# The gated unit of the S5 branch: from the end of the projection stage into the recurrence's stage, in halves of the tokens

## The chip, the cores and the metric

The kernel runs on one core of a Trainium2 chip, in fp32. The metric is the device time of one execution in microseconds; smaller is better. The core's engines are PE (matrix products), DVE (element-wise work and scans), ACT (functions and copies), POOL (element-wise work) and SP (issues most DMAs). Each engine runs its instructions strictly in order. DMAs are issued from SP's queue, and some from those of ACT and POOL.

## The reference

One layer of 1024 tokens and 2048 features. After an adaptive layer norm, a product with `w_in` makes the inputs of three branches: an S5 state space branch (512 features), a pooling branch (512) and an RWKV7 recurrence (1024, two directions). Each has a gate, and their results, times the silu of the gates, go through `w_out`, a residual and a layer norm. What the change concerns is the end of the S5 branch, cut from the reference:

```python
    y = jax.nn.gelu(y)                                  # S5 states read out
    return y * jax.nn.sigmoid(y @ w_glu + b_glu)        # the gated unit, 512 x 512
...
def _merge(ys, gates, w_out):
    return jnp.concatenate([y * jax.nn.silu(g) for y, g in zip(ys, gates)], axis=-1) @ w_out
```

## The kernel before

**Projection stage.** `in_proj` (from L644) works through feature tiles of the input product. For each tile and each of 8 slabs of the weights a load `wraw` (128 KB) is split by ACT into `whi` and by DVE into the rest `wlo`, and PE makes twelve products 128x512 into `pm`. Up to three slabs are prepared ahead. Between these products a scheduler (`Sched`, L355) lets side jobs, written as Python generators, emit their steps: S5 (`s5_run`, `s5_block`, 16 blocks in two lines), the gate of the adaptive norm, the pooling branch and, last, `s5_glu`. A small model of the engines (`Clock`, L243) tells the scheduler when the inputs of a job's next step should be there; it adds 0.45 us for each DMA to a shared clock called `hwdge`. When the products are all emitted, what is left of the side jobs follows. All of this is recorded by one helper, so the trace shows it as L300.

**The unit before** (`s5_glu_`, L1652). S5's blocks have stored y as `z_ys`, one DMA per block on ACT's queue. The unit loads `wglu` (1 MB), the bias, and y as `gluy` in 32 DMAs. For each of four feature tiles `m` it loads the gate `glug`, makes eight products, takes two sigmoids on ACT (`glus`), multiplies twice on DVE and stores `z_y` from ACT's queue.

**Recurrence stage** (`phase_c`, from L1688). A planner (`Pace`, L96) picks among jobs the one whose next instruction can start; among those that can, the smaller rank goes first. The jobs are the just-in-time preparations (rank 0), the prefixes (0.5), the solver (1), the segments (2) and the parts of the output product over the rows of `z_y` that are known (`out_first`, ranks from 0.8 to 5). A segment loads a key tile `kq` (512 KB; `KEPT` = 13 of them are held), spreads it, makes a gram on PE (`gp`), masks it on DVE (`aq`, `ar`) and stores it to `flat`. Eight segments make a batch: it is loaded as `af`, solved by 62 DVE operations (`tmp`, `nn`), and a prefix follows. The first recurrence product writes `banky`; the filler products of the output write `ofacc`. After the last recurrence product the rest of the output product (`dacc`) follows.

**Names.** `s5toep`, `s5rm`, `s5mo`, `sacc`, `s5mi`, `s5kh` are S5's tiles; `plr`, `plu`, `plinv`, `wpl` are the pooling branch's; `rvec` holds the group norm's columns and is the first load of the recurrence's stage, written after the pooling branch's store `z_y<-plr` and the unit's loads on SP.

Of the kernel before, what the change touches and what calls it, by code (L numbers as in the profile page):

```python
# [9 lines left out]
FT = mybir.dt.float32  # L10
FR = mybir.dt.float32r
I32 = mybir.dt.int32
AF = mybir.ActivationFunctionType
# [5 lines left out]
T = 1024  # L19
# [11 lines left out]
KEPT = 13  # L31
JIT = 4
# [392 lines left out]
def build(tc, A, out):  # L425

    nc = tc.nc
    with ExitStack() as ctx:
# [3 lines left out]
        def scratch(name, shape, dt=FT):  # L432
            return dram.tile(list(shape), dt, name=name)
# [5 lines left out]
        g.ys = scratch("z_ys", (32, 128, 128))  # L439
# [204 lines left out]
def in_proj(tc, A, g, psA, sched, actx):  # L644
    nc = tc.nc
    with ExitStack() as ctx:
# [475 lines left out]
        def s5():  # L1122
            yield from s5_run(tc, A, g, sched, misc, acc)
            yield
            yield from s5_glu(tc, A, g, misc)
# [129 lines left out]
GB = 2  # L1255
# [250 lines left out]
def s5_block(tc, A, g, pool, ps_tile, ps_in, st):  # L1506
# [137 lines left out]
    nc.scalar.dma_start(g.ys[gs].rearrange("g p c -> p g c"), yt)  # L1644


def s5_glu(tc, A, g, ps_tile):
    with tc.tile_pool(name="glp", bufs=1, side="right") as pool:
        yield from s5_glu_(tc, A, g, pool, ps_tile)


def s5_glu_(tc, A, g, pool, ps_tile):  # L1652

    nc = tc.nc
    w = pool.tile([128, 4, 512], FT, name="wglu")
    nc.sync.dma_start(w, A["w_glu"][0].rearrange("(k p) n -> p k n", p=128))
    bg, _ = yield from load_cols_in_steps(tc, A, g, pool, None, [(rows_of(A["b_glu"], 4), 4)], "bglu", ps_tile)
    ys = pool.tile([128, 4, 1024], FT, name="gluy")
    for q in range(32):
        r0 = 16 * (q % 8)  # L1660
        nc.sync.dma_start(ys[r0:r0 + 16, q // 8].rearrange("i (j c) -> i j c", c=128),
                          g.ys[q].rearrange("(j i) c -> i j c", i=16))
        if q % 16 == 15:
            yield 2
    yield ps_tile.one,
    for m in range(4):
        gt = pool.tile([128, T], FT, name="glug", tag="glug", bufs=1)
        nc.sync.dma_start(gt, g.gate[m * 128:(m + 1) * 128, :])
        sg = pool.tile([128, T], FT, name="glus", tag="glus", bufs=1)
        for half in range(2):  # L1670
            hs = slice(512 * half, 512 * half + 512)
            p = ps_tile()
            for k in range(4):
                nc.tensor.matmul(p, w[:, k, m * 128:(m + 1) * 128], ys[:, k, hs], start=(k == 0), stop=(k == 3))
            nc.scalar.activation(sg[:, hs], p, AF.Sigmoid, bias=bg[:, m:m + 1])
            yield ps_tile.one,
        nc.vector.tensor_tensor(sg, sg, ys[:, m], op=OP.mult)
        nc.vector.tensor_tensor(gt.rearrange("p (c j) -> p c j", j=8), gt.rearrange("p (c j) -> p c j", j=8),
                                sg.rearrange("p (j c) -> p c j", j=8), op=OP.mult)
        nc.scalar.dma_start(g.y[m * 128:(m + 1) * 128, :], gt)  # L1680
        yield ps_tile.one,
# [6 lines left out]
def phase_c(tc, A, g, out):  # L1688
    nc = tc.nc
    with ExitStack() as last, ExitStack() as ctx, ExitStack() as keys:  # L1690
# [5 lines left out]
        fin.y, fin.part, fin.hold = {}, {}, lambda: done.load >= HOLD  # L1696
# [7 lines left out]
        vec, (o_gw, o_gb) = load_cols(tc, A, g, fp, ps, [(rows_of(A["gn_w"], 8), 8), (rows_of(A["gn_b"], 8), 8)],  # L1704
                                      "rvec", lambda: mtiles[0])
# [55 lines left out]

        def seg_job(k):

            seg = allsegs[k]
            yield need("sp", 0.6, ok=lambda: done.load == k and ring.used - ring.freed < RING and k - ring.gone < KEPT)
            ring.used += 1
            kq = st.tile([128, 2, 4, 128], FT, name="kq", tag="kq", bufs=KEPT)
            nc.sync.dma_start(kq.rearrange("p a c n -> p (a c n)"), g.kq[seg.src].rearrange("p a c n -> p (a c n)"))
            t_b = seg.t_kb = P.dma(ring.out[k - KEPT] if k >= KEPT else 0.0, us=3.2)
# [544 lines left out]
        P.add(0.5, prefixes())  # L2314
        for k in range(8):
            P.add(2, seg_jobs(k))
# [394 lines left out]
```

## Time and profile before

| | us |
|---|---|
| three runs | 2967.88, 2957.72, 2965.87 |
| median | 2965.87 |
| the profiled run | 2957.1 |
| its span in the trace | 2955.3 |
| PE busy | 2653.7 (90%) |
| DVE busy | 1985.1 (67%) |
| ACT busy | 1032.9 (35%) |
| POOL busy | 1149.9 (39%) |
| DMA, mean over the span | 169 GB/s |

Shares are of the span. PE is the busiest engine, but a share over the whole span mixes stages with different limits. The trace has the start and length of each instruction, and in brackets how long its engine had been idle before it and what ended that. An fp32 product appears on PE as two records. The granted clock of PE was 0.947 of full speed on average.

### The profile page before, as it was taken

The numbers are of one execution on the slowest core, as the hardware profiler recorded it, in microseconds if no ns is written. First come the engines' busy times: TensorE is split into PE (matmuls) and PEld (weight loads), VectorE is DVE, ScalarE is ACT, GpSimd is POOL, SyncE is SP. The second block draws the span as 40 slices with busy tenths as digits, with TensorE's granted clock in tenths as the row PEclk, the third lists the DMA queues.
The fourth block names the chain that finished last, engine by engine and source line by source line (L and its number), as shares of the span: only waits on it lengthen the run. The fifth ranks groups of instructions, "written<-read, shape, count | busy, mean of one in ns | idle before, by whom it ended". The sixth has DMA issues, their size and how long they took to land. (4 is left out here: it accounts for less than half of the span.)

```text
span 2955.3 us, 56419 instructions
## 1 busy us (share of the span) xinstructions
PE 2653.7 (90%) x20080; PEld 2156.8 (73%) x20080; DVE 1985.1 (67%) x4247; ACT 1032.9 (35%) x2611; POOL 1149.9 (39%) x1681
## 2 busy tenths in 40 slices
PE   7989999999999999999899777988888899789775
PEld 2258878888888887778778366877777778678664
DVE  5548235566666567888889375677876886686568
ACT  1321224444444443222222132444443444333222
POOL 0104003343333334223552033555655556456515
PEclk9999999999999999999999877999999999798898
DMA  8734646666666665656443466665665666646744
GB/s 282 259 114 139 153 120 176 159 168 191 180 172 170 171 182 144 169 158 169 117 122 110 148 225 158 182 181 154 185 187 161 177 165 178 157 126 188 239 152 159
DMA packets 698674, 498.49 MB, mean 169 GB/s; under 512 B 347182, under 2 KB 624406, under 8 KB 695574
## 3 DMA queue, kind: packets, MB, share of 16 engines
q1 hardware_dynamic: 672632, 449.52, 54.5%
q0 software_dynamic: 6912, 24.12, 2.9%
q10 hardware_dynamic: 18848, 21.24, 2.0%
q8 instruction: 159, 2.61, 0.4%
q14 instruction: 123, 1.01, 0.1%
HBM read 339.64 MB, written 155.07 MB: 167 GB/s over the span
## 5 line engine op out<-in xcount | busy, mean ns | idle before, releaser
L300 PE MATMUL pm<-hi,whi 128*128 128x512 f32 x1600 | 511.4, 401 | 4.2 <-ACT whi L300 4.2
L300 PE MATMUL pm<-hi,wlo 128*128 128x512 f32 x1600 | 509.4, 400 | 4.3 <-DVE wlo L300 4.2
L300 PE MATMUL pm<-lo,whi 128*128 128x512 f32 x1600 | 509.2, 400 | 0.0
L300 DVE TENSOR_TENSOR wlo<-wraw,whi 128x256 fp32r<-128x256 f32 x400 | 229.2, 579 | 318.8 <-ACT whi L300 308.9
L300 PEld LDWEIGHTS pm<-hi,whi 128*128 128x128 f32 x1600 | 275.0, 190 | 58.0 <-ACT whi L300 5.8
L300 PEld LDWEIGHTS pm<-hi,wlo 128*128 128x128 f32 x1600 | 275.2, 190 | 56.1 <-DVE wlo L300 6.3
L300 PEld LDWEIGHTS pm<-lo,whi 128*128 128x128 f32 x1600 | 274.3, 189 | 51.2 <-issue 2.2
L300 ACT ACTIVATE whi<-wraw 128x256 fp32r<-128x256 f32 x400 | 160.7, 414 | 413.4 <-DMA wraw<-in_w_in 241.4
L2441 PE MATMUL ofacc<-ofhi,ofyh 128*128 128x256 f32 x768 | 250.1, 326 | 22.6 <-DVE ofev L2458 10.8
L2443 PE MATMUL ofacc<-oflo,ofyh 128*128 128x256 f32 x768 | 224.8, 293 | 3.0 <-POOL oflo L240 3.0
L2442 PE MATMUL ofacc<-ofhi,ofyl 128*128 128x256 f32 x768 | 225.1, 293 | 2.4 <-POOL ofyl L240 2.4
L1745 PE MATMUL gp<-spread,kq 128*128 128x128 f32 x1152 | 177.2, 303 | 30.5 <-ACT spread L234 12.8
L240 POOL TENSOR_TENSOR oflo<-ofw,ofhi 128x256 fp32r<-128x256 f32 x147 | 111.9, 761 | 203.2 <-ACT ofhi L234 78.0
L1745 PEld LDWEIGHTS gp<-spread,kq 128*128 128x128 f32 x1152 | 153.8, 209 | 41.5 <-DVE spread L236 12.5
L2441 PEld LDWEIGHTS ofacc<-ofhi,ofyh 128*128 128x128 f32 x768 | 153.5, 200 | 39.5 <-DVE ofev L2458 12.7
L2000 POOL TENSOR_TENSOR faded<-ping,els 64x128 f32<-64x128 f32 x304 | 127.2, 419 | 138.4 <-DVE ping L2005 125.9
L1880 DVE TENSOR_TENSOR tmp<-af,nn 128x31 f32<-128x31 f32 (+15 forms) x310 | 147.4, 476 | 22.4 <-DMA af<-flat 13.4
L1882 DVE TENSOR_TENSOR nn<-nn,tmp 128x31 f32<-128x31 f32 (+15 forms) x310 | 153.8, 496 | 10.9 <-DMA uvc<-z_v 0.2
L2442 PEld LDWEIGHTS ofacc<-ofhi,ofyl 128*128 128x128 f32 x768 | 154.7, 201 | 3.2 <-POOL ofyl L240 2.9
L2443 PEld LDWEIGHTS ofacc<-oflo,ofyh 128*128 128x128 f32 x768 | 154.4, 201 | 3.5 <-POOL oflo L240 3.5
L240 POOL TENSOR_TENSOR ofw<-ofw,ofg 128x256 f32<-128x256 f32 x143 | 115.1, 807 | 43.2 <-DMA ofw<-in_w_out 42.1
L2023 PE MATMUL banky<-ping,qt 128*128 128x128 f32 x512 | 86.9, 294 | 48.2 <-DVE ping L2005 46.4
(513 smaller groups left out, 5510.9 us busy)
## 6 DMA issues: line engine op xcount, KB each, us to landing
wraw<-in_w_in SPq DMA_DIRECT2D x400, 128.0 KB, 2.8
kq<-z_kq SPq DMA_DIRECT2D x80, 512.0 KB, 6.4
araw<-in_w_ada SPq DMA_DIRECT2D x128, 256.0 KB, 3.6
ofw<-in_w_out SPq DMA_DIRECT2D x192, 128.0 KB, 3.6
part<-ofev SPq DMA_DIRECT2D x96, 256.0 KB, 2.5
cds<-z_cd POOLq DMA_DIRECT2D x40, 512.0 KB, 5.1
z_kq<-kq SPq DMA_DIRECT2D x80, 256.0 KB, 3.1
z_kq<-kq SPq DMA_DIRECT2D x160, 128.0 KB, 3.2
```

Of the source, the lines that this page charges most:

```text
L240: (nc.vector if eng == "dve" else nc.gpsimd).tensor_tensor(out, a, b, op=op)
L300: r = x(*args, **kw)
L1745: nc.tensor.matmul(gp[:, i], seg.kb[:, i, :], qb[:, i].rearrange("p h t -> p (h t)"), start=True, stop=True)
L1880: nc.vector.tensor_tensor(tv, af[:, q, q + 1:].unsqueeze(2).to_broadcast([128, nt_, nj]), nn[:, q:q + 1, 0:nj].to_broadcast([128, nt_, nj] ...
L1882: nc.vector.tensor_tensor(nn[:, q + 1:, 0:nj], nn[:, q + 1:, 0:nj], tv, op=OP.subtract)
L2000: nc.gpsimd.tensor_tensor(to[hs], s[hs, :, hs], el[hs].to_broadcast([64, 2, 64]), op=OP.mult)
L2023: nc.tensor.matmul(b_y[:, ch.y + d], seg.qt[:, ch.c[d]], ch.s[:, d], start=(d == 0), stop=False, skip_group_check=True)
L2441: nc.tensor.matmul(o, yh[:, sl], whi, start=(first and b == 0), stop=False, skip_group_check=True)
L2442: nc.tensor.matmul(o, yl[:, sl], whi, start=False, stop=False, skip_group_check=True)
L2443: nc.tensor.matmul(o, yh[:, sl], wlo, start=False, stop=last, skip_group_check=True)
```

## The change

The unit is no longer the last side job of the projection stage. It becomes two jobs, `gated_unit(0)` and `gated_unit(1)`, of the recurrence's planner, with rank 0.4. Each works on 512 of the 1024 tokens at a time and on two of the four feature tiles `m`. Weights, y, gates and results lie in five of the thirteen key tiles: until the unit has ended (eight parts), segments from the ninth on don't load their keys. The weights of a feature tile are loaded for each half again, 8 x 256 KB in place of 1 MB. y is loaded in 4 DMAs of 256 KB a half, in runs of 64 numbers. For this `z_ys` has another layout, and each S5 block stores y with 8 DMAs (16 partitions each) in place of one. The results are stored from SP's queue. The bias joins the `rvec` load. The parts of the output product that need rows 0 to 3 of `z_y` wait until the unit's half is stored (`fin.glu`).

The diff, without the removed `s5_glu_` (shown above):

```diff
+GLUS = 5
+GLU_AT = 0.4
...
-        g.ys = scratch("z_ys", (32, 128, 128))
+        g.ys = scratch("z_ys", (512, 8, 128))
...
         def s5():
             yield from s5_run(tc, A, g, sched, misc, acc)
-            yield
-            yield from s5_glu(tc, A, g, misc)
...
-    nc.scalar.dma_start(g.ys[gs].rearrange("g p c -> p g c"), yt)
...
+    for j in range(8):
+        nc.scalar.dma_start(g.ys[16 * g0:16 * (g0 + GB), j].rearrange("(g i) c -> i g c", i=16), yt[16 * j:16 * j + 16])
...
+        glu = Seg()
+        glu.tiles = [keys_tile().rearrange("p a c n -> p a (c n)") for _ in range(GLUS)]
...
+        def glu_load(hf, t):
+            for k in range(4):
+                nc.sync.dma_start(glu.y[k].rearrange("p (j c) -> p j c", c=64),
+                                  g.ys[128 * k:128 * k + 128, :, 64 * hf:64 * hf + 64])
+                glu.t_y = P.dma(t, us=3.0)
+            glu.begun = hf + 1
+
+        def gated_unit(i):
+            w = glu.tiles[0][:, i].rearrange("p (k n) -> p k n", k=4)
+            gt, sg = (glu.tiles[3 + i][:, j] for j in range(2))
+            t_p = t_g = 0.0
+            for hf in range(2):
+                if i == 0:
+                    yield need("sp", 2.0, glu.t, ok=lambda: glu.ended == 4 * hf and done.load >= min(2, KEPT - GLUS))
+                    glu_load(hf, glu.t)
+                for m in (i, i + 2):
+                    yield need("sp", 1.0, t_p, t_g, ok=lambda: glu.begun == hf + 1)
+                    nc.sync.dma_start(w, A["w_glu"][0, :, 128 * m:128 * m + 128].rearrange("(k p) n -> p k n", p=128))
+                    t_w = P.dma(t_p, us=2.9)
+                    nc.sync.dma_start(gt, g.gate[128 * m:128 * m + 128, 512 * hf:512 * hf + 512])
+                    t_g = P.dma(t_g, us=2.9)
+                    yield need("pe", 0.95, t_w, glu.t_y, slot=misc)
+                    j, p, t = misc.take()
+                    for k in range(4):
+                        if k:
+                            yield need("pe", 0.95)
+                        nc.tensor.matmul(p, w[:, k], glu.y[k], start=(k == 0), stop=(k == 3))
+                        t_p = t = P.run("pe", 0.95, t, t_w, glu.t_y)
+                    yield need("act", 0.7, t)
+                    nc.scalar.activation(sg, p, AF.Sigmoid, bias=vec[:, o_bg + m:o_bg + m + 1])
...
+                    yield need("dve", 1.7, t, t_g)
+                    nc.vector.tensor_tensor(sg, sg, glu.y[m], op=OP.mult)
+                    by_token = gt.rearrange("p (c j) -> p c j", j=8)
+                    nc.vector.tensor_tensor(by_token, by_token, sg.rearrange("p (j c) -> p c j", j=8), op=OP.mult)
+                    t = P.run("dve", 1.7, t, t_g)
+                    yield need("sp", 0.6, t)
+                    nc.sync.dma_start(g.y[128 * m:128 * m + 128, 512 * hf:512 * hf + 512], gt)
...
+            yield need("sp", 0.6, ok=lambda: done.load == k and ring.used - ring.freed < RING and k - ring.gone < KEPT
+                       and (k < KEPT - GLUS or glu.ended == 8))
...
+        for n in range(2):
+            P.add(GLU_AT, gated_unit(n))
...
+                if row < 4:
+                    yield need("any", 0.0, ok=lambda: hf in fin.glu)
+                    t_raw = max(t_raw, fin.glu[hf])
```

The change moves instructions far beyond those it names, since the planners set the order anew. Three places follow.

DVE at the end of the projection stage, before: the last `wlo` and what stands behind it, up to the unit's first operation.

```order
1628 L300 TENSOR_TENSOR wlo<-wraw,whi 128x256
1629 L300 TENSOR_TENSOR plr<-plr 128x16x77
1630 L300 TENSOR_TENSOR plr<-plr 128x16x75
1631 L300 TENSOR_TENSOR plr<-plr 128x16x71
1632 L300 COPY bglu<-misc 128x4
1633 L300 TENSOR_TENSOR plinv<-plinv,plr 128x1024
1634 L300 TENSOR_TENSOR plu<-plinv,plu 128x1024
1635 L300 SCALAR_TENSOR_TENSOR plr<-misc,pscale,plr 128x512 x2
1636 L300 TENSOR_TENSOR glus<-glus,gluy 128x1024
```

The same engine after the change: the last `wlo` is row 1575, the pooling branch's last product is row 1638, and the rows between are S5's last blocks and the last two windows of the pooling branch.

```order
1575 L302 TENSOR_TENSOR wlo<-wraw,whi 128x256
1576 L302 SCALAR_TENSOR_TENSOR s5w<-s5m_15393,s5sin 64x640
1577 L302 TENSOR_TENSOR s5w<-s5m_15393,s5sin 64x640
...
1592 L302 TENSOR_TENSOR s5sin<-s5sin,s5w 128x640
1593 L302 TENSOR_TENSOR s5m_15624<-sacc,s5cos 128x320
...
1627 L302 SCALAR_TENSOR_TENSOR s5m_15725<-s5rm,s5m_15725 128x640
...
1637 L302 TENSOR_TENSOR plu<-plinv,plu 128x1024
1638 L302 SCALAR_TENSOR_TENSOR plr<-misc,pscale,plr 128x512 x2
1639 L493 COPY rvec<-misc_15789 128x20
```

So there were 7 rows between the last weight tile and the last product of the pooling branch, and there are 63.

SP at the start of the recurrence's stage, before: the eight key tiles of the first batch follow the unit's loads and three small ones, and the output product's loads follow them.

```order
790 L300 DMA z_y<-plr 128x1024
791 L300 DMA gluy<-z_ys 16x8x128 x16
792 L300 DMA glug<-z_gate 128x1024 x4
793 L484 DMA rvec_r<-in_gn_w 8x128
795 L1708 DMA masks<-in_k_masks 128x384
796 L1768 DMA kq<-z_kq 128x1024 x8
797 L2390 DMA ofy<-z_y 128x512
```

After: the unit's loads of y (`z_ys`), of its weights and of the gates stand behind the second key tile.

```order
794 L302 DMA z_y<-plr 128x1024
797 L486 DMA rvec_r<-in_b_glu 4x128
798 L1672 DMA masks<-in_k_masks 128x384
799 L1790 DMA kq<-z_kq 128x1024 x2
800 L1738 DMA kq<-z_ys 128x8x64 x4
801 L1755 DMA kq<-in_w_glu 128x4x128
802 L1757 DMA kq<-z_gate 128x512
803 L1755 DMA kq<-in_w_glu 128x4x128
804 L1757 DMA kq<-z_gate 128x512
805 L1790 DMA kq<-z_kq 128x1024 x6
806 L2417 DMA ofy<-z_y 128x512
```

The key tiles are still loaded in the same order, six of them behind eight other loads.

PE in the same place, before: the grams of the first segments follow the column product of `rvec`, with nothing between them but the transpositions of keys.

```order
3856 L300 MATMUL misc<-gluy,wglu 128x512 x32
3857 L489 MATMUL misc_15794<-ident,rvec_r 128x16
3858 L1827 MATMUL misc_15794<-ident,kq 128x128 x4
3859 L1745 MATMUL gp_15865<-spread_15861,kq 128x128 x4
3860 L1745 MATMUL gp_15866<-spread_15862,kq 128x128 x4
3861 L1827 MATMUL misc_15795<-ident,kq 128x128 x4
```

After: the unit's products (`misc<-kq`, 128x512) stand between the grams; row 3884 ends the first half of the tokens.

```order
3857 L1709 MATMUL gp_15861<-spread_15857,kq 128x128 x4
3858 L1849 MATMUL misc_15790<-ident,kq 128x128 x4
3859 L1764 MATMUL misc_15789<-kq 128x512 x3
3860 L1709 MATMUL gp_15862<-spread_15857,kq 128x128 x4
3861 L1764 MATMUL misc_15789<-kq 128x512
3862 L1849 MATMUL misc_15790<-ident,kq 128x128 x4
...
3875 L1764 MATMUL misc_15790<-kq 128x512 x3
3876 L1709 MATMUL gp_15862<-spread_15858,kq 128x128 x4
...
3884 L1764 MATMUL misc_15789<-kq 128x512 x4
3885 L1709 MATMUL gp_15862<-spread_15858,kq 128x128 x4
3886 L1709 MATMUL gp_15861<-spread_15857,kq 128x128 x4
```

Sixteen of the 32 products stand ahead of the last grams of the first batch, which are rows 3885, 3886, 3905 and 3906.

## Rows read from the trace of the kernel before

**Rows 1.** The page's costliest groups: busy us, mean ns, idle before.

```profile
L300 PE MATMUL pm<-hi,whi 128*128 128x512 f32 x1600 | 511.4, 401 | 4.2 <-ACT whi L300 4.2
```

**Rows 2.** Windows: length, busy of PE, PEld, DVE, ACT, POOL, clock, DMA.

```profile
1642.80:1689.10 46.30, 34.35 (x68) 13.71 (x68) 12.30 (x10) 7.70 (x10) 1.55 (x4) 0.85 0.40 124
1689.10:1739.00 49.90, 32.48 (x213) 31.03 (x213) 23.89 (x41) 17.08 (x41) 15.31 (x18) 0.76 0.86 271
1739.00:1832.60 93.60, 67.75 (x741) 61.60 (x741) 71.95 (x165) 21.68 (x46) 36.95 (x52) 0.78 0.62 170
1832.60:2770.00 937.40, 820.02 (x10792) 717.69 (x10792) 675.23 (x1668) 379.35 (x1062) 527.87 (x960) 0.93 0.63 171
```

**Rows 3.** Timeline of the unit's stretch: start, us, engine, line, operation.

```profile
1633.16 0.42 DVE L300 TENSOR_TENSOR wlo<-wraw,whi 128x256 fp32r<-128x256 f32 x1 [1.85 <-ACT whi L300]
...
1640.09 0.19 PE L300 MATMUL misc<-ident,bglu_r 4*128 4x4 f32 x1 [1.46 <-DMA bglu_r<-in_b_glu]
...
1659.41 27.14 PE L300 MATMUL misc<-gluy,wglu 128*128 128x512 f32 x58 [1.68 <-DMA gluy<-z_ys]
...
1687.72 1.23 DVE L300 TENSOR_TENSOR glus<-glus,gluy 128x1024 f32<-128x1024 f32 x1 [1.76 <-ACT glus L300]
1689.11 0.31 SPq L484 DMA_DIRECT2D rvec_r<-in_gn_w  x1
...
1690.27 6.35 SPq L1768 DMA_DIRECT2D kq<-z_kq  x8
1692.15 1.90 DVE L300 TENSOR_TENSOR glug<-glug,glus 128x1024 f32<-128x1024 f32 x1 [3.20 <-DMA glug<-z_gate]
```

**Rows 4.** Timeline of PE's side work in the projection, at three places.

```profile
1485.35 1.25 PE L300 MATMUL sacc<-s5u,s5mt 128*128 128x160 f32 x8
...
1591.33 0.60 PE L300 MATMUL misc<-ident,s5mi 128*128 128x128 f32 x4
...
1591.77 1.35 PE L300 MATMUL misc<-s5fc__15113,s5mi 128*128 128x16 f32 x12
...
1630.28 0.38 PE L300 MATMUL misc<-s5u,s5toep 128*128 128x128 f32 x2
...
1631.53 0.71 PE L300 MATMUL pm<-lo,whi 128*128 128x512 f32 x2
...
1642.92 1.98 PE L300 MATMUL misc<-plu,wpl 128*128 128x512 f32 x4
```

**Rows 5.** Windows up to 1645.7, all and `wlo` alone; timeline at 1625.

```profile
1565.19:1645.70 80.51, 78.59 (x367) 63.28 (x365) 68.23 (x89) 22.18 (x36) 19.25 (x17) 1.00 0.45 131
...
1565.19:1645.70 80.51, 29.66 (x96) 18.01 (x96) 11.01 (x22) 1.00 0.45 131
...
1624.75 0.82 DVE L300 SCALAR_TENSOR_TENSOR s5w<-s5m,s5sin 64x640 f32<-64x640 f32 x1
1625.56 1.56 POOL L300 TENSOR_TENSOR s5rm<-s5m,s5cos 128x640 f32<-128x640 f32 x1
1625.59 2.22 DVE L300 TENSOR_TENSOR s5w<-s5m,s5sin 64x640 f32<-64x640 f32 x1
```

**Rows 6.** The tile `z_ys`: ns of one issue, minimum, median, maximum.

```profile
L300 ACTq DMA_DIRECT2D z_ys<-s5y x16: 367/381/431, 1164.7 to 1632.2; - x16
```

**Rows 7.** DMA issues from 1685 to 1760: KB each, median us to landing.

```profile
kq<-z_kq SPq DMA_DIRECT2D x19, 512.0 KB, 7.2
...
flat<-aq SPq DMA_DIRECT2D x12, 64.0 KB, 2.5
```

**Rows 8.** Timeline of the recurrence's start, as in group 3.

```profile
1724.31 0.69 DVE L1750 TENSOR_TENSOR aq<-gp,masks 128x512 f32<-128x512 f32 x1 [0.91 <-PE gp L1745]
...
1734.19 0.34 SPq L1860 DMA_DIRECT2D af<-flat  x1
...
1739.05 0.18 DVE L1880 TENSOR_TENSOR tmp<-af,nn 128x31 f32<-128x31 f32 x1
```

**Rows 9.** The tile `ofacc` alone, window from 2770 to 2831, columns as above.

```profile
2770.00:2831.00 61.00, 20.77 (x150) 19.17 (x150) 5.45 (x8) 0.86 0.72 233
```

More of the change, by code (lines that the diff above doesn't have):

```diff
@@ L1643, in s5_block @@
     ps_tile.drop(po)
-    nc.scalar.dma_start(g.ys[gs].rearrange("g p c -> p g c"), yt)
[L1647 to L1681, printed above, removed]
+    for j in range(8):
+        nc.scalar.dma_start(g.ys[16 * g0:16 * (g0 + GB), j].rearrange("(g i) c -> i g c", i=16), yt[16 * j:16 * j + 16])
 class Seg:
@@ L1695, in phase_c @@
         fin = Seg()
-        fin.y, fin.part, fin.hold = {}, {}, lambda: done.load >= HOLD
+        fin.y, fin.part, fin.glu, fin.hold = {}, {}, {}, lambda: done.load >= HOLD
         out_first(tc, A, g, last, P, fin)
@@ L1702, in phase_c @@
         ps = ctx.enter_context(tc.tile_pool(name="cps", bufs=1, space=PSUM))
-        vec, (o_gw, o_gb) = load_cols(tc, A, g, fp, ps, [(rows_of(A["gn_w"], 8), 8), (rows_of(A["gn_b"], 8), 8)],
-                                      "rvec", lambda: mtiles[0])
+        vec, (o_gw, o_gb, o_bg) = load_cols(tc, A, g, fp, ps, [(rows_of(A["gn_w"], 8), 8), (rows_of(A["gn_b"], 8), 8),
+                                                               (rows_of(A["b_glu"], 4), 4)], "rvec", lambda: mtiles[0])
         els, bon = g.els, g.bon
@@ L1760, in diagonal, with keys_tile @@
             return aq.rearrange("p s c n -> p (s c) n")[r0:r0 + 32, :, c0:c0 + 32]
+        def keys_tile():
+            return st.tile([128, 2, 4, 128], FT, name="kq", tag="kq", bufs=KEPT)
+        glu = Seg()
+        glu.tiles = [keys_tile().rearrange("p a c n -> p a (c n)") for _ in range(GLUS)]
+        glu.t = 0.0
+        glu.y = [glu.tiles[1 + k // 2][:, k % 2] for k in range(4)]
+        glu.begun = glu.ended = 0
+        def glu_load(hf, t):
[4 more added lines that the diff above has]
+            glu.begun = hf + 1
@@ new lines, in gated_unit @@
+        def gated_unit(i):
[21 more added lines that the diff above has]
+                    nc.scalar.activation(sg, p, AF.Sigmoid, bias=vec[:, o_bg + m:o_bg + m + 1])
+                    t = P.run("act", 0.7, t)
+                    misc.give(j, t)
+                    yield need("dve", 1.7, t, t_g)
[5 more added lines that the diff above has]
+                    nc.sync.dma_start(g.y[128 * m:128 * m + 128, 512 * hf:512 * hf + 512], gt)
+                    t_g = P.dma(t, us=2.9)
+                    glu.t = max(glu.t, t_g)
+                    glu.ended += 1
+                    if glu.ended % 4 == 0:
+                        fin.glu[hf] = glu.t
@@ L1762, in seg_job @@
         def seg_job(k):
             seg = allsegs[k]
-            yield need("sp", 0.6, ok=lambda: done.load == k and ring.used - ring.freed < RING and k - ring.gone < KEPT)
+            yield need("sp", 0.6, ok=lambda: done.load == k and ring.used - ring.freed < RING and k - ring.gone < KEPT
+                       and (k < KEPT - GLUS or glu.ended == 8))
             ring.used += 1
-            kq = st.tile([128, 2, 4, 128], FT, name="kq", tag="kq", bufs=KEPT)
+            kq = keys_tile()
             nc.sync.dma_start(kq.rearrange("p a c n -> p (a c n)"), g.kq[seg.src].rearrange("p a c n -> p (a c n)"))
-            t_b = seg.t_kb = P.dma(ring.out[k - KEPT] if k >= KEPT else 0.0, us=3.2)
+            t_b = seg.t_kb = P.dma(ring.out[k - KEPT] if k >= KEPT else glu.t, us=3.2)
```

## The prediction

> **What bounds the kernel now.** I read the table of windows first, cut at the last product of the projection (1642.8 us), at the first load of the recurrence's stage (1689.1), at the first operation of its solve (1739.0) and at the first product of the recurrence proper (1832.6). Up to 1642.8 the projection is bound by PE: in the whole stage its products waited only 4.2 us for a weight tile [rows 1]. Then come 46.3 us in which the gated unit runs alone: PE is busy for 34.35 us of them, DVE for 12.30 and the DMA engines at 0.40 [rows 2]. The 143.5 us after that start the recurrence: PE is busy 32.48 of 49.9 and 67.75 of 93.6 us, DVE 71.95 of those 93.6, the DMA engines 0.86 in the first part. The recurrence itself is bound by PE, 820.02 of 937.4 us [rows 2]. So there is idle PE time where the change puts the unit, but it lies in a chain of loads, grams, masks, stores and a solve that runs link by link; the timeline of that chain and of the 46.3 us came next, and the order of instructions of both programs last.
>
> The timeline of the gated unit shows what frees the recurrence's stage. SP issues in order, so that its first load stands behind the unit's last gate load (rvec at 1689.11, key tiles from 1690.27), while PE works through 58 of the unit's 64 matmul records in 27.14 us [rows 3].
>
> **The gated unit leaves.** With it go the 46.3 us from 1642.8 to 1689.1, if nothing else is late there. Something is, and the order shows it, not the diff's intent: S5's y now leaves through 8 stores a block instead of one, the planner of the side jobs charges each DMA of a job, and so it puts S5's last blocks later. Behind the last weight tile's `wlo` DVE had 7 rows left up to the pool branch's last product; now it has 63.
>
> **The tail on DVE (first term).** The products end sooner, because side work has left their stretch on PE. Moved behind the last product are three output blocks (1.25 us each, from the start at 1630.28 to the next product at 1631.53), two groups of eight records into `sacc` (1.25 each), one transposition group with its kernel taps (from 1591.33, 0.60, to the end of the 1.35 at 1591.77, 1.8) and two `plu,wpl` products (1.98) [rows 4]: 3.75 + 2.5 + 1.8 + 1.98 = 10.0 us. The bias's transposition, at which PE stood 1.46 us at 1640.09 [rows 3], is gone too, some 2 us with the pause before it. So the products end at 1642.8 - 12 = 1630.8, and the last `wlo`, which came 9.6 us before that end, 2 of them the pause (1633.16 in [rows 3]), comes at about 1623.5.
>
> What then stands on DVE is what stood in the last 80.5 us before: from 1565.19 to 1645.70 DVE was busy 68.23 us, 11.01 of them with `wlo` [rows 5], which leaves 57.2. It no longer hides under products. To it I add some 9 us for hand-overs: the tail has two whole blocks of S5, each of which waits for `sacc`, for a small kernel `s5kh` and for POOL, and POOL's share stretches DVE: the same 64x640 operation took 0.82 us at 1624.75 and 2.22 at 1625.59, beside a POOL operation of 1.56 us [rows 5]. Bounds: 0 (the 68.23 us hold such stretches already) to 16 (POOL's 19.25 us in that window, nearly all in DVE's way). The last pool product is then ready at 1623.5 + 57.2 + 9 = 1689.7. SP's queue holds its store, the three small loads and the masks (0.3 to 0.4 us each, as at 1689.11 to 1690.27) ahead of the first key tile, so that it is issued at about 1691.5 against 1690.27 [rows 3]: **+1.2**, with bounds of -10 and +12. The whole 46.3 us are taken by the tail.
>
> **S5's stores on ACT's queue (second term).** Each of 16 blocks now issues eight stores instead of one; an issue took 0.381 us in the median [rows 6], so a block holds ACT 7 x 0.38 = 2.7 us longer, and 13 of 16 blocks come before the last weight tile, whose copies ACT makes: 13 x 2.7 = 35 us of ACT time, in a stage with copies three sets ahead. A set lasted 80.51 / 22 = 3.66 us on average in [rows 5], so the cover is some 11 us and a burst of 3 us fits under it. If the cover is gone (the copies sit behind a store that waits for an earlier one), all 35 show. I take **+3**, nearest to the 4.2 us that the stage waits now [rows 1], between 0 and 35.
>
> The Trainium skill, DMA: Bandwidth & Descriptors, section Rules for kernel authors, wants small transfers joined, since under 64 KB one pays mostly overhead; its section Specifications asks for runs of at least 512 B. Against both, the change stores 16 KB pieces and reads y back in 256-byte runs. The rows here show 64 KB in 128-byte runs landing in 2.5 us and 512 KB in 4096-byte runs in 7.2 [rows 7]: a 256 KB load of y would land in some 4 us at the second rate and in 10 at the first, an estimate. By the rule the sum would be 6 us higher, by the row of long runs it stays.
>
> **The start of the recurrence (third term).** The unit has rank 0.4, ahead of the solver's 1 and the segments' 2, so its first half stands between the grams of the first eight segments. Before, the first key tile was issued at 1690.27, the eighth mask began at 1724.31, the solve's input was loaded at 1734.19 and the solve began at 1739.05 [rows 8]: 48.8 us from the first issue. Now:
> - SP issues eight more loads right behind the second key tile and four more, with three stores, ahead of the first flat store: for the eight 8 x 0.4 = 3.2 us of issue and 2 MB more, at the 271 GB/s of that stretch [rows 2] 7.4 us.
> - On PE 16 of the unit's 32 products stand ahead of the last grams of the batch. 58 records, or 29 products, took 27.14 us [rows 3], 0.94 each: 15 us. PE was idle 17.4 of 49.9 us there, but mostly while it waited for keys, and it will now wait for the unit's loads in the same order.
> - On DVE five pairs come before the first operation of the solve. A pair took 1.23 + 1.90 us on 1024 tokens [rows 3], about 1.6 on half: 8 us. The stores of the unit's results stand ahead of the flat stores on SP, too.
> These partly overlap. PE's 15 alone is the lower reading, PE and DVE together 23 the upper; I take **+20**. Bounds: -10, because 12 triples of `ofacc` (36 products) leave this stage and the unit may fit wholly in idle time; +45, if the two tiles' units run in series, each with a load, four products, a sigmoid, a pair and a store, as 46.3 us did before. Nothing behind hides it: the solve, the second batch and the prefix follow link by link until 1832.6.
>
> **The end (fourth term).** `ofacc` products were a filler. By the order 48 more of them now come behind the last product of the recurrence. From 2770 to 2831 150 of them took 20.77 us [rows 9], 0.138 each: 48 x 0.138 = **+6.6**. Bounds -5 (PE idles there while the last pairs are finished) and +10 (twice the rate at the lower clock, less some idle).
>
> **Sum.** 1.2 + 3 + 20 + 6.6 = 30.8. The profiled run took 2957.1 us (span 2955.3), which gives 2987.9. The runs shown have a median of 2965.87 and reach from 2957.72 to 2967.88, so the profiled one is at the lower edge; I forecast **2988 us**.
>
> **Rivals.**
> A. The forecast: the tail fills the gap and the recurrence starts late. Own range 2970 to 3020.
> B. The start hides the unit (third term 0 to 5), the tail as forecast: -5 to +9, so 2952 to 2966. For it speak the 17.4 idle PE us at the start and DVE's 26 idle; against it that products, masks and flat stores of the first batch stand behind the unit's on three engines in order.
> C. Faster: the tail doesn't take the gap, because DVE is through with S5 soon after the products. Then the 46.3 us are gained, less a third term of 0 to 20: -26 to -46, or 2911 to 2931. For it: 46.3 us are truly taken out, and PE is busy only two thirds of the start. Against it: 57.2 us of DVE work in one stretch behind a last `wlo` that comes late because the products set its time.
> D. Much slower: ACT's bursts of stores starve the products, the whole 35 us show, on top of A's other terms: 2957.1 + 28 + 35 = 3020. For it: each store of a burst waits for a free place behind earlier ones; against it the 11 us of cover.
> The change then does what it says, and in A it does so only by halves: the unit leaves the gap, and S5 fills it.
>
> **Chances.** A 0.60, B 0.18, C 0.14, D 0.08. About 0.3%, 9 us, is what a measurement of this kernel can tell from no change. Faster by more than that: C and a little of B, 0.17. Within: most of B and the low edge of A, 0.17. Slower: 0.66. The range of 2950 to 3025 leaves C out, 14 in 100, and some of D.
>
> **What would show it.** Right: DVE is busy almost without a break for over 55 us behind the last `wlo`, while PE is nearly idle; the first key tile is issued some 60 us after the last projection product; the solve's first operation comes about 70 us after the first key tile, not 48.8; PE's work between the last recurrence product and the end grows by some 7 us. Wrong: the first key tile comes before 1670 us (C), the solve begins within 52 us of it (B), or waits for `whi` reach tens of us in the projection (D).

## The result, and the profile after

The changed kernel took 2995.68 us in the median of four runs (2985.34 to 3001.57), the kernel before 2961.8 (2953.28 to 2967.88). The ratio is 1.0116, with a 95% interval from 1.0091 to 1.0141: slower by some 34 us. The profiled run took 2996.86 us, 39.8 more than the profiled run before.

Five marks in each trace show where they went: the start of the last product of the projection, the first key tile's issue, the first operation of the solve, the first product of the recurrence, and the start of the last copy of its results. Each column is the difference of two such starts, from marks rounded to 0.1 us; the last reaches to the end of the span. The forecast's +3 for the stores belongs to no one column.

| us | last product at | to first key tile | to solve | to recurrence | to its last result | to the end | span |
|---|---|---|---|---|---|---|---|
| before | 1642.4 | 47.9 | 48.7 | 93.6 | 935.9 | 186.8 | 2955.3 |
| after | 1628.6 | 66.0 | 66.2 | 102.2 | 937.1 | 194.9 | 2995.0 |
| forecast of the difference | -12.0 | +13.2 | +20 | 0 | 0 | +6.6 | |
| difference | -13.8 | +18.1 | +17.5 | +8.6 | +1.2 | +8.1 | +39.7 |

First the windows of the changed kernel, cut at the same marks (length, then busy time of PE, PEld, DVE, ACT and POOL, the granted clock, the DMA share and GB/s).

```profile
1628.90:1694.60 65.70, 22.36 (x77) 16.13 (x75) 54.74 (x59) 4.05 (x6) 19.24 (x17) 0.61 0.26 70
1694.60:1760.80 66.20, 53.47 (x253) 37.43 (x253) 27.66 (x44) 15.63 (x31) 23.47 (x26) 0.82 0.82 236
1760.80:1863.00 102.20, 70.70 (x668) 60.70 (x668) 71.84 (x144) 27.36 (x61) 34.24 (x45) 0.76 0.64 187
```

The first row answers to the unit's 46.30 us in [rows 2]. There PE was busy 34.35 us and DVE 12.30; now DVE is busy 54.74 of 65.70 and PE 22.36. The stretch is emptied of the unit and filled with S5. Its timeline (start, us, engine, line, operation, and in brackets the idle time before) has the last weight tile, the end of the products, an output block of S5 for which PE stood 17 us, the pooling branch's last product and the first key tile:

```profile
1621.98 1.78 DVE L302 TENSOR_TENSOR wlo<-wraw,whi 128x256 fp32r<-128x256 f32 x1
...
1628.41 0.62 PE L302 MATMUL pm<-hi,wlo 128*128 128x512 f32 x2
...
1680.63 1.22 PE L302 MATMUL misc<-s5rm,s5mo 128*128 128x128 f32 x4 [17.12 <-DVE s5rm L302]
...
1691.16 0.75 DVE L302 SCALAR_TENSOR_TENSOR plr<-misc,pscale,plr 128x512 f32<-128x512 f32 x1 [0.96 <-PE misc L302]
...
1694.62 0.82 SPq L1790 DMA_DIRECT2D kq<-z_kq  x2
1695.49 5.23 SPq L1738 DMA_DIRECT2D kq<-z_ys  x4
...
1760.79 0.19 DVE L1902 TENSOR_TENSOR tmp<-af,nn 128x31 f32<-128x31 f32 x1 [2.82 <-DMA af<-flat]
...
1863.01 1.22 PE L2045 MATMUL banky<-ping,qt 128*128 128x128 f32 x4 [2.94 <-DVE ping L2027]
```

In [rows 3] the last `wlo` started at 1633.16 and the first key tile at 1690.27, in [rows 8] the solve at 1739.05. The tail behind the last `wlo` lasts 70 us up to the pool's last product; from 1623.8 to 1691.9 DVE is busy for 59.76 us. The four loads of y take SP 5.23 us to issue, from 0.53 to 2.95 each. The eight key tiles before took 6.35 in [rows 3].

The stores of y, which were one row of 381 ns in the median [rows 6], and what waited for them, from the view of that tensor:

```profile
L302 ACTq DMA_DIRECT2D z_ys<-s5y x128: 309/434/1291, 1162.3 to 1686.8; - x128
L1738 SPq DMA_DIRECT2D kq<-z_ys x8: 530/772/2948, 1695.5 to 1744.9; - x8
...
  ACT whi L302: 65.6, 11
```

ACT stood 65.6 us, in eleven places, with a weight tile's copy behind a burst of stores. Little of it reached PE: its products on weight tiles waited 9.3 us for `whi` and 7.5 for `wlo` in the whole run, against 4.2 and 4.2 before. The products even ended 13.8 us sooner than before, since much of S5's work had left their stretch.

### The profile page after: what moved, and what is told of

Same layout as the page of the kernel before. It is cut to its first block, busy times and chain, and to the rows that moved or that the text cites. A ratio compares the mean times of both kernels' runs of the same rounds, so it can differ in the third digit from the quotient of the medians.

```text
span 2995.0 us, 56458 instructions
## 1 busy us (share of the span) xinstructions
PE 2676.6 (89%) x20079; PEld 2173.6 (73%) x20079; DVE 1979.1 (66%) x4243; ACT 1027.7 (34%) x2602; POOL 1171.2 (39%) x1688
## 4 chain that ended last, share of the span: by engine, by line
PE 60%; DVE 18%; DMA 9%; SPq 4%; issue 4%; POOL 2%; ACT 2%; ACTq 0%; DVEq 0%; POOLq 0%
PE pm L302 31%; PE misc L302 5%; PE pc L302 4%; PE gp L1709 4%; DVE tmp L1902 3%; PE ada L302 3%; DVE nn L1904 3%; SPq L302 2%; PE ofacc L2468 2%; DMA kq<-z_kq 1%; DVE ping L2027 1%; PE ofacc L2469 1%; PE ofacc L2470 1%; PE banky L2045 1%; DVE pre L242 1%
## 5 line engine op out<-in xcount | busy, mean ns | idle before, releaser
L242 POOL TENSOR_TENSOR ofw<-ofw,ofg 128x256 f32<-128x256 f32 x140 | 115.2, 824 | 41.3 <-DMA ofw<-in_w_out 39.7
```

The lines of the kernel that those rows point to most:

```text
L242: (nc.vector if eng == "dve" else nc.gpsimd).tensor_tensor(out, a, b, op=op)
```

## The experiments

All times are medians; the ratio is to the kernel before on the same chip, whose median was 2961.33 us in the first group, 2960.95 in the second, 2959.37 in the third and 2958.25 in the last. The stages are those of the table above.

| run | us | ratio, interval | last product at | to first key | to solve | to recurrence | to last result | to the end |
|---|---|---|---|---|---|---|---|---|
| e1_s5_on_time | 2977.43 | 1.0054, 1.0032 to 1.0077 | 1668.6 | 6.4 | 66.2 | 102.6 | 928.7 | 195.3 |
| e2_unit_later | 2981.66 | 1.0068, 1.0042 to 1.0094 | 1668.6 | 6.6 | 43.8 | 83.0 | 989.9 | 186.0 |
| e3_stores_alone | 3012.65 | 1.0174, 1.0147 to 1.0202 | 1628.9 | 113.3 | 48.9 | 91.9 | 941.1 | 187.9 |
| e4_stores_on_time | 2992.31 | 1.0111, 1.0087 to 1.0136 | 1677.1 | 45.0 | 47.9 | 90.9 | 950.6 | 188.0 |
| e5_two_stores | 2954.15 | 0.9976, 0.9962 to 0.9989 | 1631.2 | 24.9 | 66.2 | 104.3 | 935.4 | 193.4 |
| e6_before_two_stores | 2954.71 | 0.9978, 0.9961 to 0.9994 | 1628.7 | 58.3 | 47.9 | 91.4 | 941.2 | 186.4 |
| e7_before_four_loads | 2953.24 | 0.9983, 0.9963 to 1.0003 | 1630.1 | 52.0 | 48.6 | 93.2 | 948.6 | 188.1 |
| e8_quarter_products | 2954.93 | 0.9977, 0.9958 to 0.9997 | 1627.1 | 24.6 | 65.1 | 100.4 | 929.8 | 194.1 |
| e9_keys_first | 2927.75 | 0.9893, 0.9873 to 0.9913 | 1629.6 | 24.9 | 70.3 | 101.8 | 936.6 | 165.5 |
| e10_after_two_masks | 2959.53 | 1.0002, 0.9984 to 1.002 | 1629.1 | 24.9 | 70.1 | 104.5 | 926.9 | 194.5 |
| e11_before_filled | 2979.31 | 1.0076, 1.0048 to 1.0104 | 1629.0 | 57.5 | 46.2 | 93.2 | 990.3 | 161.1 |
| e12_after_filled | 2945.53 | 0.9948, 0.9926 to 0.997 | 1632.9 | 24.5 | 66.4 | 103.7 | 957.9 | 160.6 |

**Is the late S5 the planner's doing, and is it the whole of the tail?** The first run leaves the changed kernel as it is but lets the planner count one store of eight:

```diff
     for j in range(8):
-        nc.scalar.dma_start(g.ys[16 * g0:16 * (g0 + GB), j].rearrange("(g i) c -> i g c", i=16), yt[16 * j:16 * j + 16])
+        (nc.scalar if j == 0 else nc.scalar.inner).dma_start(g.ys[16 * g0:16 * (g0 + GB), j].rearrange("(g i) c -> i g c", i=16), yt[16 * j:16 * j + 16])
```

> The changed kernel, but the planner of the side jobs counts the eight y stores of an S5 block as one DMA. By the order S5's blocks then stand where they stood before (7 rows on DVE between the last weight tile and the pooling branch's last product), and everything from the first key tile on is in the changed kernel's order, row for row. My theory (the tail of S5 took the gap): the first key tile is issued near 1650 us in place of 1694.6, the solve still starts some 66 us after it, and the kernel takes about 2950 us, 40 to 48 less than the changed kernel. Rival 1 (the planner's charge was right: the bursts hold up ACT, which already waited 72.2 us for earlier y stores): the products wait for weight tiles by tens of us, and the time is 2970 or more. Rival 2 (the tail is hidden in any case, the late start of the recurrence is all): the time stays near 2990.

S5 came on time and the tail was gone: 6.4 us from the last product to the first key tile. But the last product came at 1668.6 us, 40 later than in the changed kernel and 26 later than before. The time fell by 18 us and not by 40 to 48. Rival 1 holds in part: the charge stood for a real cost.

The same two states were tried on the kernel before, without moving the unit: the layout of y, eight stores and 32 loads of y, then the same with one store counted (by the edit above).

```diff
-        g.ys = scratch("z_ys", (32, 128, 128))
+        g.ys = scratch("z_ys", (512, 8, 128))
...
-    nc.scalar.dma_start(g.ys[gs].rearrange("g p c -> p g c"), yt)
+    for j in range(8):
+        nc.scalar.dma_start(g.ys[16 * g0:16 * (g0 + GB), j].rearrange("(g i) c -> i g c", i=16), yt[16 * j:16 * j + 16])
...
-        nc.sync.dma_start(ys[r0:r0 + 16, q // 8].rearrange("i (j c) -> i j c", c=128),
-                          g.ys[q].rearrange("(j i) c -> i j c", i=16))
+        nc.sync.dma_start(ys[r0:r0 + 16, q // 8].rearrange("i (j c) -> i j c", c=128), g.ys[16 * q:16 * q + 16])
```

> The kernel before with nothing changed but the layout of y and its eight stores a block (the unit stays behind the projection, with 32 loads of 16 partitions). By the order S5 falls behind as in the changed kernel. My theory (the stores alone make S5 late): the tail of about 60 us and the unit's stretch of about 46 stand one after the other, less 12 us by which the products end sooner and some of the unit's loads under the tail: 2990 to 3010 us. Rival (S5 is late only because the unit left the job): no change, 2955 to 2965.

> As the run before, but the planner counts the eight stores of a block as one, so that the order of S5 is that of the kernel before. What is left is the price of 112 more issues on ACT's queue and their waits. My theory: +0 to +6 us against the kernel before. Rival (bursts starve the projection): +20 to +40 us, with the idle time of PE before products on weight tiles up from 4.2 us to over 25.

The stores alone cost 51 us when they are counted, and 31 when they are not. The first was foreseen in kind (first key tile at 1742.22, tail and unit one after the other), and 3012.65 us lies a little above the expected range. The second was not: my +0 to +6 fell, and the rival's +20 to +40 came. Its sign was to be PE's idle time before products on weight tiles, over 25 us; on `whi` and `wlo` together the page counts 17.8. In PE's waits the greater growth is at S5's own products, from 10.3 us in eight waits for `s5rm` to 24.7 in eleven; that DVE came to S5's operations later because its weight tiles were late is argued, not shown. The timeline of ACT in that run shows a burst, one store and then seven:

```profile
1591.89 0.32 ACTq L300 DMA_DIRECT2D z_ys<-s5y  x1
1592.24 4.91 ACTq L1645 DMA_DIRECT2D z_ys<-s5y  x7
1597.20 1.03 ACT L300 ACTIVATE whi<-wraw 128x256 fp32r<-128x256 f32 x3 [5.34 <-DMA z_ys<-s5y]
```

The 5.34 us of idle time before the copies are the burst itself. Three weight tiles were copied back to back behind it: they had been due. The waits of ACT from 1160 to 1690 us in the same run (total, number, longest):

```profile
ACT whi L300 <- DMA z_ys<-s5y: 76.7, 13, 7.5
```

Why does a burst last so long? The semaphore events of the trace tell: SP's and ACT's DMAs share eight semaphores, and a burst of eight stores goes through all of them. In the changed kernel the 16 bursts last 85.8 us in all. In 30.7 us of that, at 35 stores, ACT stood until the semaphore had counted an earlier DMA as landed, and in 33 of the 35 places that was a load issued by SP, not a store of y. With two stores a block there are three such places, 5.8 us. No run changed the semaphores alone.

**Is it the number of stores or the layout?** The changed kernel, and the kernel before with the new layout, with one store for each of the block's two groups:

```diff
-    for j in range(8):
-        nc.scalar.dma_start(g.ys[16 * g0:16 * (g0 + GB), j].rearrange("(g i) c -> i g c", i=16), yt[16 * j:16 * j + 16])
+    for x in range(GB):
+        nc.scalar.dma_start(g.ys[16 * (g0 + x):16 * (g0 + x) + 16].rearrange("i j c -> j i c"), yt[:, x])
```

> The changed kernel, but a block of S5 stores y with two DMAs (one for each of its two groups, 64 KB each, the same layout of y) in place of eight. The planner counts both. My theory now (the eight stores hold ACT up by some 5 us a block, and whether the planner counts them only decides if that shows as products that wait or as a late S5): the products end at 1640 to 1650 us, the first key tile is issued at 1648 to 1660, the solve starts 66 us after it, and the time is 2945 to 2962 us, 15 to 32 below the run with S5 on time. Rival (it is the layout, runs of 512 bytes to 16 places, not the number of stores, that costs): ACT's waits for earlier y stores stay above 40 us and the time near 2975.

> The kernel before with the new layout of y and two stores a block; the unit stays behind the projection. My theory: 0 to +8 us against the kernel before, 2960 to 2970. Rival (the layout costs by itself): +20 or more, as with eight stores.

It is the number. With two stores the planner counts both and makes S5 only a little late, and the stall is mostly gone. The view of the tensor in the first of these runs:

```profile
L302 ACTq DMA_DIRECT2D z_ys<-s5y x32: 577/587/1156, 1167.6 to 1635.4; - x32
...
  ACT whi L302: 14.9, 6
```

14.9 us of waits against 65.6. The layout costs the kernel before nothing: 0 to +8 us were expected, and it got 0.22% faster. The first run was expected between 2945 and 2962 and took 2954.15, 41 us below the changed kernel; the products ended sooner than expected (1631.2).

These two runs answer the question of the move itself. They differ in the unit alone, its place and its form (halves, weights loaded twice, y in 4 loads a half), and they are equal (2954.15 and 2954.71). The stretch to the first key tile is 33.4 us shorter. Then the solve starts 18.3 later against that tile and the recurrence another 12.9: the first product of the recurrence starts at the same time in both:

```profile
1826.58 0.71 PE L2045 MATMUL banky<-ping,qt 128*128 128x128 f32 x4 [2.94 <-DVE ping L2027]
```

```profile
1826.26 0.71 PE L2023 MATMUL banky<-ping,qt 128*128 128x128 f32 x4 [0.18 <-DVE ping L2005]
```

The first row is the changed kernel with two stores, the second the kernel before with two. All that leaves the gap comes back before the first product.

**What makes the start late?** The first try put the unit behind the segments (on the kernel with S5 on time):

```diff
-GLU_AT = 0.4
+GLU_AT = 2.2
```

> As the run before, and the unit has rank 2.2 in place of 0.4: eight key tiles are loaded before its loads, and the first batch's masks, stores and solve come before its work on DVE. My theory (the unit held up the start link by link): the solve starts 50 us after the first key tile in place of 66, and the time falls by a further 12 to 20 us to about 2935. Rival (the start is set by the second batch, whose keys now come even later, or by PE's work in sum): the solve starts earlier but the first product of the recurrence does not, and the time stays within 5 us of the run before.

The solve started 43.8 us after the first key tile, and the recurrence's first product 41.8 us sooner than in the run with S5 on time. So it is the unit's place ahead of the batch's work that makes the start late. But the recurrence grew by 61 us. Rows of that run, from SP and ACT: the unit's last store, the load of the second batch's input to the solve, and the first result of the second pair.

```profile
1824.19 0.34 SPq L1776 DMA_DIRECT2D z_y<-kq  x1
...
1864.13 0.34 SPq L1882 DMA_DIRECT2D af<-flat  x1
...
1969.80 0.57 ACT L2089 ACTIVATE outs<-banky 64x128 f32<-64x128 f32 x2 [0.97 <-PE banky L2081]
```

In the run with S5 on time the load was at 1814.20 and the second pair's first result at 1962. Keys from the ninth segment on wait for the unit's tiles, so a late unit makes the second pair late: it began 8 us later although the first began 42 sooner, which makes 50 of the 61. I had written the rival with the first product unmoved; it moved, and the second pair took its place.

What of the unit holds up the start? A quarter of its products, on the changed kernel with two stores:

```diff
-                        nc.tensor.matmul(p, w[:, k], glu.y[k], start=(k == 0), stop=(k == 3))
+                        if k == 0:
+                            nc.tensor.matmul(p, w[:, k], glu.y[k], start=True, stop=True)
```

> As the run with two stores, but the unit makes only the first of the four products of each sum (8 in place of 32), so its result leaves out three quarters of the contraction; order, loads, sigmoids, multiplications and stores stay. My theory (PE's 15 us of products ahead of the batch's last grams are most of the late start): the solve starts 50 to 56 us after the first key tile, and the time is 8 to 16 us below that run. Rival (loads and hand-overs in order set the start: 2 MB ahead of six key tiles, and ACT and DVE standing behind the unit): 60 us or more, and within 6 us of that run.

65.1 us against 66.2, and the same total within its scatter: not the products, though the next stretch, to the recurrence, shrank by 3.9 us. This falls on my third term, whose largest part they were. So the loads: the eight key tiles ahead of the unit's first loads and then two masked key tiles too, as the mark from which the unit may load. Both stand on the changed kernel with two stores; the first edit, and the second:

```diff
-                    yield need("sp", 2.0, glu.t, ok=lambda: glu.ended == 4 * hf and done.load >= min(2, KEPT - GLUS))
+                    yield need("sp", 2.0, glu.t, ok=lambda: glu.ended == 4 * hf and done.load >= min(8, KEPT - GLUS))
```

```diff
-                    yield need("sp", 2.0, glu.t, ok=lambda: glu.ended == 4 * hf and done.load >= min(2, KEPT - GLUS))
+                    yield need("sp", 2.0, glu.t, ok=lambda: glu.ended == 4 * hf and done.mask >= 2)
```

> As the run with two stores, but the unit's first loads wait for the eighth key tile in place of the second, so that all eight key tiles of the batch are issued ahead of the unit's 2 MB. My theory (loads ahead of six key tiles and the waits behind them, not products, make the late start): the solve starts 52 to 60 us after the first key tile in place of 66.2, and the time is 4 to 12 us below that run, 2942 to 2950. Rival (the work of all engines in that stretch is what it is, and only its order changes): within 3 us of that run, with the solve 64 to 68 us after the first key tile.

> As the run with two stores, but the unit's first loads wait for the second mask of the batch, so that the first output loads (on which ACT stood 6.3 us in the run with a quarter of the products) are ahead of the unit's loads, too. My theory: the solve starts 50 to 58 us after the first key tile, and since the unit still ends before the second batch's keys are wanted, 6 to 15 us come out of the total. Rival (the second pair of the recurrence waits for the second batch, whose keys wait for the unit's end, as in the run with the later unit): the first pair starts sooner and the second does not, and the total stays within 4 us of that run.

Neither brought the solve forward (70.3 and 70.1 us after the first key tile). That theory fell, too. ACT's copies, for which I had named a wait of 6.3 us, are no more than one link.

But both edits move the loads of the unit's first half only; the marks are long passed when the second half begins. Rows of the changed kernel, from DVE and SP, show what the second half does: the last mask of the first batch, the first of the eight loads, and behind the eight the batch's last four stores.

```profile
1744.93 0.69 DVE L1714 TENSOR_TENSOR aq<-gp,masks 128x512 f32<-128x512 f32 x1 [0.20 <-PE gp L1709]
```

```profile
1742.58 4.33 SPq L1738 DMA_DIRECT2D kq<-z_ys  x4
...
1751.56 2.44 SPq L1819 DMA_DIRECT2D flat<-aq  x4
```

The mask was done at 1745.62 and its stores began at 1751.56, 5.9 us later. In the kernel before the eighth mask began at 1724.31 [rows 8] and the stores behind it at 1726.79. In the run with two masks the same eight loads, with three stores, stand ahead of them from the mask's end at 1704.80 to 1714.67, 9.9 us. So the order of the second half's loads is a rival that no run tested.

What is shown is that the unit as a whole, standing among the first batch's instructions on queues in order, makes the start late by some 18 us, whatever its products or the order of its first loads; how much each link gives stays open. For the next 9 to 13 us the cause stays open, too. In the changed kernel eight pairs of the unit's operations stand on DVE (`kq<-kq`) between 1719 and 1790 (1.7 to 2.8 us each), three of them behind the solve's start at 1760.79. But with the unit behind the segments four pairs stand in that stretch, and it lasts 83.0 us, less than in the kernel before.

**Why then was the run with keys first the fastest of all?** It has 2927.75 us, 26 below the run with two stores, and all of it at the end: 165.5 us against 193.4. The output product's fillers behind the last result, first in the run with two stores, then in that with keys first (tile `ofacc` alone):

```profile
2762.00:2955.40 193.40, 30.98 (x209) 29.76 (x208) 6.69 (x10) 0.83 0.54 180
```

```profile
2763.20:2928.70 165.50, 14.62 (x90) 13.75 (x90) 2.74 (x4) 0.84 0.55 186
```

90 of them were left and not 209. Between the first product and the last result the same view counts 1926 of them against 1821: the planner had put some 105 more into the recurrence, which did not grow for it (936.6 against 935.4 us): PE's idle time in it fell from 118.9 to 104.9 us. A changed wait sent the planner another way. To see whether that is to be had at will, with the unit in either place, the filling of each step was raised:

```diff
-QUOTA = 0.8
+QUOTA = 1.0
```

The first run has the unit behind the projection, the second inside the recurrence's stage, both with two stores.

> The kernel before with two stores a block, and the planner of the recurrence fills each step with 1.0 us of other work in place of 0.8 (QUOTA). By the order no output product (ofacc) is then left behind the last recurrence product, against 162. My theory (the run with keys first gained 28 us because 90 of these products were left there and not 210; its start was no sooner): the time from the last recurrence result to the end falls from 186 to some 155 us, the recurrence stays within 8 us of 936, and the kernel takes 2920 to 2935 us without moving the unit at all. Rival (the gain of that run came of the order of its loads, not of what is left at the end): no more than 5 us below the run with two stores alone, 2950 to 2958, because the recurrence grows by what the end loses.

> The changed kernel with two stores a block and the same setting of 1.0 us; no output product is left behind the last recurrence product, against 210. With the end alike in this run and the one before it, the two differ in the place of the unit alone. My theory: the same end of some 155 us, so that the move's own worth shows: with the filled end it takes 0 to 12 us less than the run before it (the two runs with two stores were equal, while the changed one had 7 us more at the end). Rival (the move itself is worth the 46 us of the stretch that it took away): 25 us or more below the run before it.

Half right. The end fell to 161 us in both, with none left. But the recurrence grew, by 49 us with the unit behind the projection and by 22 with it inside: in the first run by more than the end lost, so that its 2979.31 us lie above both forecasts. The windows of the recurrence tell part of the difference. In the first run PE was busy 36.0 us longer than with 0.8 us of filling, for 163 more records, and its granted clock was 0.90 against 0.92; in the second 26.9 us longer for 203 more records, at 0.93 as with 0.8 us. PE's idle time gives the rest: it grew by 13.1 us in the first and fell by 4.4 in the second. Why stays open. By its number (34 us less than the run before it) the second run meets its rival, but I don't read this as the worth of the move: filling and clock differ in each.

**The unit where it was, with four loads of y**, on the kernel before with two stores:

```diff
-    for q in range(32):
-        r0 = 16 * (q % 8)
-        nc.sync.dma_start(ys[r0:r0 + 16, q // 8].rearrange("i (j c) -> i j c", c=128), g.ys[16 * q:16 * q + 16])
-        if q % 16 == 15:
-            yield 2
+    yield 2
+    for k in range(4):
+        nc.sync.dma_start(ys[:, k].rearrange("p (j c) -> p j c", c=128), g.ys[128 * k:128 * k + 128])
+    yield 2
```

> As the run before, and the unit behind the projection loads y with 4 DMAs of 512 KB in place of 32 of 16 partitions, which the new layout allows. In the kernel before PE waited 9.3 us in three waits for those loads and reached its 58 back-to-back records 16 us after the first two. My theory: the unit's stretch falls from 46 to some 33 us, and the kernel takes 2945 to 2955 us, below the kernel before. Rival (the gates' loads, one tile at a time, set the stretch: SP's four took 32 us): the stretch stays above 42 us and the time does not fall.

The stretch to the first key tile went from 58.3 to 52.0 us. The total lies in the forecast range, but it did not fall measurably against the run before it (2954.71). SP's row of the last three gates' loads in this run:

```profile
1659.18 21.75 SPq L300 DMA_DIRECT2D glug<-z_gate  x3
```

One tile at a time, they set most of the stretch; the rival is nearer.

## Why the prediction was right

The forecast was 2988 us, and slower by 22 to 31 us; 34 came. The account of the tail was right. That the sum came so near is in part luck: a start sized from the wrong parts and a missed delay of the same order stand in it. Point by point:

- **The tail** was read from the order and sized from [rows 4, 5]. The last product began at 1628.6 us (its end was forecast at 1630.8), the last `wlo` began at 1621.98 (1623.5), the pool's last product ended at 1691.9 (1689.7), and the first key tile was issued at 1694.62 (1691.5): +4.3 against +1.2. The 57.2 us of DVE work with 9 for hand-overs became 59.8 and some 8, both counted behind the last `wlo`.
- **The stores on ACT** were the step that was wrong in kind. I took +3 beside the tail, with the copies' lead as cover, and gave 0.08 to bursts that starve the products. The bursts last some 5 us and not 3. With S5 on time they cost 31 us. With S5 late ACT's waits before `whi` reach 65.6 us, tens of us as in rival D's sign, and the products are still not late: PE itself waited 16.8 us for `whi` and `wlo`, against 8.4 before. The sign should have named PE's waits. Nor do the stores wait for a place behind the earlier ones of their burst, as D has it, but in 33 of 35 places for loads of SP. The stores are no separate term: the tail and the 35 us that I had as the upper bound are two forms of one cost, which two stores a block take away together, and alone the stores cost 31 us even if the planner counts one of eight.
- **The start** was +17.5 against +20, from the wrong parts. I made it of products (15 us), loads and pairs on DVE. Three quarters of the products give 1 us of it, and the order of the first half's loads nothing; the second half's loads ahead of the last four flat stores, which I had not counted, stand in the trace.
- **Missed:** +8.6 us between the solve's start and the first product, where I wrote that nothing behind hides a late start. Three of the unit's last four pairs on DVE lie behind the solve's start, but no run shows that they are the cause.
- **The end** was +8.1 against +6.6. The rate of 0.138 us a product is too low: the 48 more made 0.17 us each. Between other runs it is no constant: 119 fewer took away 27.9 us with keys first, 0.23 each, and the 209 gone from the filled run took away 32.8, 0.16 each.
- **Rival B**, that the start hides the unit, is refuted by the runs with two stores: where nothing else is late, it takes back 31.2 of the 33.4 us. Its own sum was wrong as well: with the tail, the stores and the end as forecast and a start of 0 to 5 it gives +10.8 to +15.8, not -5 to +9. **Rival C** was out, but for S5 on time its 46 us would not have come either.

## What to carry to other kernels

When a piece of work moves to a place with idle engine time, look first at what its new neighbours queue behind, and at what takes its old place: here the eight stores a block, which were only there to serve the move, cost 41 us, and the move without them brought nothing measurable. Count DMA issues on an engine that also feeds another: eight small stores held ACT for 5 us, two of the same bytes for about one. And where a planner sets the order, a small edit changes filling far away: compare the stages of the traces before crediting a gain to the edit, as with the 2927.75 us of the run with keys first, which is the version to keep (1.07% below the kernel before) though its gain lies at the end and not at the start that it was meant to bring forward.

## What the runs showed of the hardware

A store that waits costs its engine the wait, not its issue alone. In the changed kernel the eight stores of a block were issued at 434 ns in the median, in place of 381 for one of eight times the bytes, and a burst took 5.4 us in the mean, 1.9 of them waits for earlier DMAs to land, most of them loads from SP's queue. A load of 256 KB in 256-byte runs took SP 0.53 to 2.95 us to issue, 0.77 in the median; the first two of 512 KB in long runs took 0.82 together. The one such 256 KB load whose landing the trace tells took 6.3 us, between the 4 and the 10 that the prediction estimated. The Trainium skill, DMA: Bandwidth & Descriptors, section Rules for kernel authors, has transfers under 64 KB as mostly overhead. What the traces show beside it is the issuing engine's part, not the transfer's own: the same bytes in two stores of 64 KB left 14.9 us of ACT's waits, in eight of 16 KB 65.6.
